# Transposed queries and keys: a pair of heads on the partitions instead of one head in both directions

## The chip, the cores and the metric

The kernel runs on one core of a Trainium2 chip. The metric is the device time of one execution in microseconds, the median of several runs. The engines are TensorE (PE: matmuls and transposes, with its weight loads, PEld, beside them), VectorE (DVE), ScalarE (ACT), GpSimd (POOL) and SyncE (SP), which issues most of the DMAs.

## The reference

One layer of an encoder over 2048 positions with 1024 features, float32. One projection feeds two groups of heads. Group A is gated linear attention with four heads (64 key dimensions, 128 value dimensions), run in both directions over chunks and summed; group B is latent attention with a softmax over all positions. Their outputs are gated, joined, projected and normalised with the residual. What the change touches is the linear attention:

```python
# log_a, one for each direction d in (fwd, bwd):
log_a = log_sigmoid(lr_d @ wg2_d + bg_d) / 16          # (B, S, 4, 64)
def gla_chunked(q, k, v, log_a, strict):               # bwd: on flipped inputs, strict
    b = cumsum(log_a)                                  # inside a chunk of positions
    q_dec, k_dec = q * exp(b), k * exp(-b)
    k_tail = k * exp(b_last - b)
    attn = where(mask, einsum('bhtd,bhsd->bhts', q_dec, k_dec), 0)
    o_intra = attn @ v
    # scan over chunks:
    o_inter = q_dec @ state
    state = state * exp(b_last)[..., None] + einsum('bhsd,bhsv->bhdv', k_tail, v)
    return o_intra + o_inter
o = rms_norm(o_fwd + flip(o_bwd)) * silu(gate)
```

## The kernel before

The kernel has four stages in time: a first sweep over the sequence (`sweep_a`, to about 368 us), a second sweep (`sweep_c`), the softmax attention over four blocks of 512 queries, and the output projection with the norm. Every product of two float32 matrices is made of three matmuls on split values: a high part, written by a ScalarE copy (`hi`, L362 to L367) or a VectorE one, and a low part, a subtraction (`lo`, L369 to L371); `mm3` (L417 to L421) issues high x high, high x low, low x high at lines 419, 420 and 421.

The first sweep takes the 2048 positions in 16 chunks of 128, from the last (c=15, step i=0) to the first (c=0, i=15). For both directions at once it makes the decayed queries and keys of a chunk, its inner attention and its contribution to the state. The order of a chunk's work:

- Products (`products`, tile ipa): the chunk's x against 1056 columns in three groups of 288, 384 and 384 (low rank and q; k and part of v; the rest of v), eight pieces of k-depth 128 each, three matmuls a piece.
- `ga_lr`: the two ScalarE copies and the VectorE subtraction that make the low-rank input lr from the first group; `ga_q2`, `ga_k2`: ScalarE copies of q and k from PSUM.
- `ga_lrT` (L863 to L869): PE transposes lr, ScalarE copies it (lrTs). `ga_z` (L874 to L893): four matmuls make the log decay z (L881), ScalarE (L885, L887, L889) and VectorE (L891) make za of it.
- `ga_sums`: two scans on VectorE (L902 forward, L904 backward) sum za along the chunk, small copies (L908 to L911) take the sums at the chunk's middle and end (cl), L914 subtracts the middle, and ScalarE takes the exponentials E1 (L918) and E2 (L920). `ga_cw` (L924) takes the exponential of cl.
- `ga_q`: PE transposes q (qT, L933), VectorE multiplies by E1 (qd, L936), a DMA stores qd for the second sweep (L937), and by halves of the partitions qd is split into qbh and qbl, each 64 partitions x 512. `ga_k`: kT (L952), kd (L955), its parts kh and kl.
- `ga_kt`: four PE transposes of kd (kt, L969) and the parts kth and ktl. `ga_intra`: the attention scores Ap, chosen by direction into At (ScalarE L986, VectorE L988), its parts Ah and Al. `ga_av`: Op, and oi, stored (L1010). `ga_state`: Up (L1021, L1022), Us (ScalarE L1025, VectorE L1027, GpSimd L1029), stored as su_s (L1030), then the running state Sb (L1035). `ga_bst`: Sm (L1050), stored (L1051).
- Gates (`gate_products`, tile ipg, 512 columns; gs on ScalarE and VectorE) for all chunks but 15, 14 and 0, whose gates come elsewhere.

How work is ordered: chunk i=0 runs in program order. For i=1 to 3 an order written out by hand (`ORDER_A`) holds on all engines. From i=4 a table places stages behind pieces of the products:

```python
STEPS_A = {(0, 4): [("q", "prev"), ("k", "prev")], (1, 3): [("kt", "prev"), ("lrT", "cur")],
           (1, 5): [("z", "cur"), ("cw", "cur")], (1, 7): [("intra", "prev")], (2, 3): [("state", "prev")],
...
```

So q and k of the chunk before are transposed after the fifth piece of the first product group, kt and lrT stand after the fourth piece of the second group, z two pieces later; within this a scheduler of the framework may shift instructions of an engine. The last chunk has its own order at the end of `sweep_a`. PSUM tiles come from three pools of two buffers: ip (ipa, ipg), gp (z, Ap, Op) and tr (transposes and Up). The stores of chunks 0 and 1 (`STORE_POOL`) are issued by GpSimd, all others by SyncE. After the sweep SyncE loads the weights and constants of the second one (L1140), and qd_s, su_s, oi_s and u_s are read back from DRAM chunk by chunk (SU, qdb, oib, ub), which then feed GpSimd's Sf and SU and the matmuls Ob (L1417, L1418).

In all tiles of a direction and head the partitions hold (direction r, dimension d) and the free axis the head h; q and k are copied twice side by side (q2, k2), so that one 128x128 transpose of a head gives it for both directions.

Of the kernel before, what the change touches and what calls it, by code (L numbers as in the profile page):

```python
# [9 lines left out]
F32 = mybir.dt.float32  # L10
F32R = mybir.dt.float32r
I32 = mybir.dt.int32
AF = mybir.ActivationFunctionType
ALU = mybir.AluOpType
# [4 lines left out]
P = 128  # L19
# [4 lines left out]
H = 4  # L24
# [6 lines left out]
TAU_INV = 1.0 / 16.0  # L31
# [323 lines left out]
class K:  # L355
# [413 lines left out]
        yield  # L769

    def ga_q2(self, d):
        d["q2"] = d["g1"].tile([P, H, 2, 64], F32, tag="q2", name=f"q2_{d['c']}", bufs=2)
        self.hi(d["q2"], d["pt", 0][:, 32:288].rearrange("p (h o d) -> p h o d", h=H, o=1).to_broadcast([P, H, 2, 64]))
        yield

    def ga_k2(self, d):
        d["k2"] = d["g1"].tile([P, H, 2, 64], F32, tag="k2", name=f"k2_{d['c']}", bufs=2)
        self.hi(d["k2"], d["pt", 1][:, 0:256].rearrange("p (h o d) -> p h o d", h=H, o=1).to_broadcast([P, H, 2, 64]))
        yield

    def ga_v1(self, d):
# [114 lines left out]
    def ga_sums(self, d):  # L896

        nc, c, za, rmask = self.nc, d["c"], d["za"], d["rmask"]
        V, Ac = nc.vector, nc.scalar
        b = self.t512(d, "E1")  # L900
        f2 = lambda t: t.rearrange("p h t -> p (h t)")
        V.tensor_tensor_scan(f2(b)[0:64], f2(rmask)[0:64], f2(za)[0:64], 0.0, ALU.mult, ALU.add)  # L902
        yield
        V.tensor_tensor_scan(f2(b)[64:128, ::-1], f2(rmask)[64:128, ::-1], f2(za)[64:128, ::-1],  # L904
                             0.0, ALU.mult, ALU.add)
        yield
        cl = d["cl"] = d["g1"].tile([P, 3, H], F32, tag="cl", name=f"cl{c}")
        V.tensor_copy(cl[0:64, 0], b[0:64, :, 63])  # L908
        V.tensor_copy(cl[64:128, 0], b[64:128, :, 64])
        V.tensor_copy(cl[0:64, 2], b[0:64, :, 127])  # L910
        V.tensor_copy(cl[64:128, 2], b[64:128, :, 0])  # L911
        V.tensor_tensor(cl[:, 1], cl[:, 2], cl[:, 0], ALU.subtract)
        yield
        d["zdone"] = V.tensor_tensor(b, b, cl[:, 0, :, None].to_broadcast([P, H, P]), ALU.subtract).ins  # L914
        yield
        E2 = self.t512(d, "E2")
        d.update(E1=b, E2=E2)
        Ac.activation(E2, b, AF.Exp, scale=-TAU_INV)  # L918
        yield
        Ac.activation(b, b, AF.Exp, scale=TAU_INV)  # L920
        yield

    def ga_cw(self, d):
        self.nc.scalar.activation(self.cw[:, d["c"]], d["cl"], AF.Exp, scale=TAU_INV)  # L924
        yield

    def ga_q(self, d):

        nc, c = self.nc, d["c"]
        qbh, qbl = d["qbh"], d["qbl"]  # L930
        qT = d["tr"].tile([P, H, P], F32, tag="tr", name=f"qT{c}")
        for h in range(H):
            nc.tensor.transpose(qT[:, h], d["q2"][:, h].rearrange("p a d -> p (a d)"), self.ident)  # L933
        yield
        qd = self.t512(d, "qd")
        nc.vector.scalar_tensor_tensor(qd, qT, 0.125, d["E1"], ALU.mult, ALU.mult)  # L936
        self.store(c).dma_start(self.qd_s[c], qd.rearrange("p h t -> p (h t)"))  # L937
        yield
        halves = (slice(0, 64), 0), (slice(64, 128), 1)
        for r, j in halves:  # L940
            self.hi(qbh[r, :, j], qd[r])
            yield
        for r, j in halves:
            self.lo(qbl[r, :, j], qd[r], qbh[r, :, j])
            yield

    def ga_k(self, d):

        nc, c = self.nc, d["c"]
        kT = d["tr"].tile([P, H, P], F32, tag="tr", name=f"kT{c}")  # L950
        for h in range(H):
            nc.tensor.transpose(kT[:, h], d["k2"][:, h].rearrange("p a d -> p (a d)"), self.ident)  # L952
        yield
        kd = d["kd"] = self.t512(d, "kd")
        nc.vector.tensor_tensor(kd, kT, d["E2"], ALU.mult)  # L955
        yield
        kh = d["kh"] = self.t512(d, "kh", dt=F32R)
        self.hi(kh, kd)
        yield
        kl = d["kl"] = self.t512(d, "kl", dt=F32R)  # L960
        self.lo(kl, kd, kh)
        yield

    def ga_kt(self, d):

        nc, c = self.nc, d["c"]
        kt = d["tr"].tile([P, H, P], F32, tag="tr", name=f"kt{c}")
        for h in range(H):
            nc.tensor.transpose(kt[:, h], d["kd"][:, h], self.ident)  # L969
        yield  # L970
        kth = d["kth"] = self.t512(d, "kth", dt=F32R)
        self.hi(kth, kt)
        yield
        ktl = d["ktl"] = self.t512(d, "ktl", dt=F32R)
        self.lo(ktl, kt, kth)
        yield

    def ga_intra(self, d):

        nc, c = self.nc, d["c"]  # L980
        Ap = d["gp"].tile([P, H, 2, P], F32, tag="gp", name=f"Ap{c}")
        for h in range(H):
            self.mm3(Ap[:, h], d["kh"][:, h], d["kl"][:, h], d["qbh"][:, h], d["qbl"][:, h])
        yield
        At = self.t512(d, "At")
        nc.scalar.activation(At, Ap[:, :, 1], AF.Copy)  # L986
        yield
        nc.vector.copy_predicated(At, d["mask"][:, None, :].to_broadcast([P, H, P]), Ap[:, :, 0])  # L988
        yield
        Ah = d["Ah"] = self.t512(d, "Ah", dt=F32R)  # L990
        self.hi(Ah, At)
        yield
        Al = d["Al"] = self.t512(d, "Al", dt=F32R)
        self.lo(Al, At, Ah)
        yield
# [949 lines left out]
def layouts(inputs):  # L1945

    g = {k: np.asarray(v) for k, v in inputs.items()}
# [3 lines left out]
    q, k, v, gate, lrf, lrb, cq, ckv, kr, mg = (slice(cols[i], cols[i + 1]) for i in range(10))  # L1951
    cat = lambda *s: np.concatenate([w[:, t] for t in s], axis=1)
    a = {}
# [2 lines left out]
    a["wA"] = cat(lrf, lrb, q, k, v).reshape(NK, P, NA)  # L1956
    a["wB"] = cat(gate, cq, ckv, kr, mg).reshape(NK, P, 1472)
    a["wO"] = g["w_out"][0].reshape(NK, P, D)
    wg = np.zeros((32, H, 2, 64), np.float32)
    wg[0:16, :, 0] = g["gla_wg2_fwd"][0].reshape(16, H, 64)  # L1960
    wg[16:32, :, 1] = g["gla_wg2_bwd"][0].reshape(16, H, 64)
    bg = np.stack([g["gla_bg_fwd"][0].reshape(H, 64), g["gla_bg_bwd"][0].reshape(H, 64)], axis=1)
    wg, bg = wg.reshape(32, H * P), bg.reshape(1, H * P)
    a["wg"] = np.concatenate([wg, wg, wg, bg, bg], axis=0)
    wgm = np.zeros((98, 1), np.float32)
# [17 lines left out]
    a["ident"] = np.eye(P, dtype=np.float32)  # L1983
    a["mask"] = np.triu(np.ones((P, P), np.int32))
    rmask = np.ones((P, H, P), np.float32)
    rmask[0:64, :, 0] = 0.0
    rmask[64:128, :, P - 1] = 0.0
    a["rmask"] = rmask
    invf = (10000.0 ** (-np.arange(32) / 32)).astype(np.float32)
    a["invf"] = np.broadcast_to(invf[None, :], (P, 32))  # L1990
# [20 lines left out]
```

## Time and profile before

| | |
|---|---|
| median of 3 runs | 1307.95 us (1307.42 to 1308.66) |
| the profiled execution | 1308.66 us |
| its span, first to last instruction | 1306.3 us |
| mean granted TensorE clock | 0.997 |
| instructions | 19979 |
| busy: PE, PEld | 1280.9 us, 1130.9 us |
| busy: DVE, ACT, POOL | 958.2, 812.8, 783.6 us |

The page's times are microseconds unless marked ns. A row of a group reads: line, engine, operation, out<-in by the program's names, partitions x elements, x count, then busy time and mean ns of one, then the idle time of the engine just ahead of them and what ended it. Rows of the timeline and of the chain of waits start with the start time and the duration. In a row of the waits stand who waited, for whom, the total in us, how often and the longest. Matmuls are pipelined and their ends are modelled, so neighbours on PE overlap.

### The profile page before, as it was taken

How to read it: one execution, taken by the hardware profiler on the slowest of the kernel's cores; microseconds unless marked ns; L12 is line 12 of the kernel's file. 1: busy time of each engine (PE TensorE's matmuls, PEld its weight loads, DVE VectorE, ACT ScalarE, POOL GpSimd, SP SyncE). 2: the span in 40 equal slices, each digit the busy share in tenths (PEclk: the TensorE clock that was granted, in tenths of full speed). 3: DMA queues.
4: the chain of work that ended last, by engine and by line, in shares of the span. 5: the costliest groups of instructions: out<-in, count | busy, mean ns of one | idle time of the engine just before them, and what ended most of it. 6: DMA issues, size and time to landing. Idle time of an engine off the chain costs nothing.

```text
span 1306.3 us, 19979 instructions
## 1 busy us (share of the span) xinstructions
PE 1280.9 (98%) x7081; PEld 1130.9 (87%) x7081; DVE 958.2 (73%) x1712; ACT 812.8 (62%) x1339; POOL 783.6 (60%) x494
## 2 busy tenths in 40 slices
PE   7999999999999999999999999999999999999997
PEld 7999999999989999999788888888888887887786
DVE  6967774645675455555798888888888888377998
ACT  6764656655575656655688878888888888411110
POOL 0143333242457666672298888889999999934441
PEclk9999999999999999999999999999999999999999
DMA  8131313122475565565501111122123110376563
GB/s 285 61 101 54 94 49 91 55 68 79 132 249 170 193 214 181 178 210 170 145 1 41 41 42 41 41 57 65 58 81 97 41 41 12 119 234 175 195 197 109
DMA packets 107820, 145.81 MB, mean 112 GB/s; under 512 B 17251, under 2 KB 62695, under 8 KB 107721
## 3 DMA queue, kind: packets, MB, share of 16 engines
q1 hardware_dynamic: 99128, 142.41, 35.6%
q0 software_dynamic: 672, 2.10, 0.4%
q8 instruction: 56, 0.92, 0.3%
q10 hardware_dynamic: 7920, 0.03, 0.3%
q14 instruction: 44, 0.35, 0.2%
HBM read 94.14 MB, written 50.36 MB: 111 GB/s over the span
## 4 chain that ended last, share of the span: by engine, by line
PE 83%; DMA 4%; DVE 3%; ACT 2%; POOL 1%; issue 1%; SPq 1%; DVEq 0%; POOLq 0%; ACTq 0%
PE pS L1520 4%; PE o L419 4%; PE o L420 4%; PE o L421 4%; PE pS L1522 4%; PE pS L1523 4%; PE pS L1521 4%; PE pS L1524 4%; PE ipa L419 4%; PE ipa L421 4%; PE ipa L420 4%; PE pz L420 2%; PE pz L419 2%; PE pz L421 2%; PE ipg L419 2%; PE ipg L420 2%
## 5 line engine op out<-in xcount | busy, mean ns | idle before, releaser
L371 POOL TENSOR_TENSOR pl<-s,ph 128x1024 fp32r<-128x1024 f32 x128 | 306.5, 2414 | 58.3 <-ACT ph L365 54.5
L1542 DVE TENSOR_TENSOR rm<-pS,rm 128x512 f32<-128x512 f32 x210 | 144.8, 690 | 36.5 <-ACT s L1529 31.2
L1529 ACT ACTIVATE s<-pS 128x1024 f32<-128x1024 f32 x128 | 131.4, 1027 | 60.6 <-PE pS L1524 51.3
L1566 DVE TENSOR_TENSOR s<-s,mb 128x1024 f32<-128x1024 f32 x128 | 151.2, 1213 | 9.5 <-PE mb L1560 9.3
L1029 POOL TENSOR_TENSOR Us<-Us,cw 128x512 f32<-128x512 f32 x16 | 18.5, 1157 | 227.2 <-DVE Us L1027 175.3
L365 ACT ACTIVATE ph<-s 128x1024 fp32r<-128x1024 f32 x128 | 135.2, 1057 | 17.1 <-PE o L421 16.5
L1570 ACT ACTIVATE s<-s 128x1024 f32<-128x1024 f32 x128 | 131.4, 1050 | 13.7 <-DVE s L1566 13.7
L419 PE MATMUL ipa<-wah,xah 128*128 128x384 f32 (+1 forms) x384 | 131.1, 342 | 6.7 <-ACT wah L365 6.7
L421 PE MATMUL ipa<-wah,xal 128*128 128x384 f32 (+1 forms) x384 | 125.5, 327 | 0.0
L420 PE MATMUL ipa<-wal,xah 128*128 128x384 f32 (+1 forms) x384 | 125.2, 326 | 0.0
L1520 PE MATMUL pS<-qh,ckvT_h 128*128 128x512 f32 x256 | 102.6, 401 | 0.8 <-DVE rm L1542 0.4
L419 PE MATMUL o<-ph,vh 128*128 128x512 f32 x256 | 101.0, 395 | 0.0
L421 PE MATMUL o<-ph,vl 128*128 128x512 f32 x256 | 99.8, 390 | 0.0
L1522 PE MATMUL pS<-qh,ckvT_l 128*128 128x512 f32 x256 | 99.8, 390 | 0.0
L1523 PE MATMUL pS<-rh,krs 128*128 128x512 f32 x256 | 99.8, 390 | 0.0
L1524 PE MATMUL pS<-rl,krs 128*128 128x512 f32 x256 | 99.7, 389 | 0.0
L1521 PE MATMUL pS<-ql,ckvT_h 128*128 128x512 f32 x256 | 99.7, 389 | 0.0
L420 PE MATMUL o<-pl,vh 128*128 128x512 f32 x256 | 99.7, 389 | 0.0
L1593 DVE TENSOR_TENSOR ap<-ap,s 128x512 f32<-128x512 f32 x120 | 83.0, 692 | 2.7 <-ACT s L1570 0.7
L371 POOL TENSOR_TENSOR ol<-of,oh 128x512 fp32r<-128x512 f32 x32 | 42.9, 1343 | 66.9 <-ACT oh L365 66.9
L419 PEld LDWEIGHTS ipa<-wah,xah 128*128 128x128 f32 x384 | 73.7, 192 | 7.9 <-ACT wah L365 7.0
L419 PE MATMUL pz<-xch,wzh 128*128 128x256 f32 x256 | 74.8, 292 | 0.0
(325 smaller groups left out, 3858.0 us busy)
## 6 DMA issues: line engine op xcount, KB each, us to landing
xcf<-xT_dram SPq DMA_DIRECT2D x16, 512.0 KB, 4.9
xr<-x_dram SPq DMA_DIRECT2D x16, 512.0 KB, 6.6
out_dram<-rr SPq DMA_DIRECT2D x32, 256.0 KB, 2.0
xaf<-xT_dram SPq DMA_DIRECT2D x14, 512.0 KB, 4.2
oib<-oi_s SPq DMA_DIRECT2D x16, 256.0 KB, 4.4
qdb<-qd_s SPq DMA_DIRECT2D x16, 256.0 KB, 4.6
SU<-su_s SPq DMA_DIRECT2D x16, 256.0 KB, 4.9
ub<-u_s SPq DMA_DIRECT2D x16, 256.0 KB, 4.7
```

What stands on the lines that cost most here:

```text
L365: return nc.scalar.activation(dst, src, AF.Copy).ins
L371: return e.tensor_tensor(dst, src, hi.bitcast(F32), ALU.subtract).ins
L419: mm(out, ah, bh, start=start, stop=False)
L420: mm(out, ah, bl, start=False, stop=False)
L421: mm(out, al, bh, start=False, stop=stop)
L1520: mm(ps[:, e], kh, qh, start=True, stop=False)
L1521: mm(ps[:, e], kh, ql, start=False, stop=False)
L1522: mm(ps[:, e], kl, qh, start=False, stop=False)
L1523: mm(ps[:, e], kr, rh, start=False, stop=False)
L1524: mm(ps[:, e], kr, rl, start=False, stop=True)
L1542: V.tensor_tensor(d["rm"], src[:, e], d["rm"], ALU.max)
L1566: V.tensor_tensor(s, s, d["mb"][:, None, :].to_broadcast([P, 2, QB]), ALU.subtract)
```

## The change

The partitions of the transposed tiles now hold (head g of a pair, dimension d), and the free axis (direction r, pair q). q2 and k2 are copied once, 256 elements a partition instead of 512, and q and k take two transposes of 128x128 each instead of four. qd and kd multiply by the decay of both directions by reading the two transposed tiles twice. The scans become one per direction over 128 partitions and 256 elements instead of 64 partitions and 512; the small copies have 128x2 instead of 64x4. What is read by the stages behind has its old layout: the exponentials of cl are written by four ScalarE instructions of 64 partitions x 6 (with other partitions in than out) instead of one of 128 x 12, qd is stored by four DMAs (64 partitions, two runs of 512 bytes each) instead of one (128 partitions, 2 KB each), kth and ktl are written in another order of their four blocks of 64, and Ap is read by direction. The four transposes of kd stay. The weights wg and bias bg and the mask of the scans are laid out accordingly in the host's preparation.

In the built programs PE has 64 matmul instructions fewer, ScalarE 48 instructions more, SyncE 42 and GpSimd 6 DMA issues more. The order on each engine is otherwise the same but for a few places: from i=4 on one product matmul (L419) stands between kt and lrT on PE; ScalarE issues two cw, E2, two cw, E1, Us in place of cw, Us, E2, E1; GpSimd issues the four stores of chunk 0's qd ahead of Sm.

```diff
@@ -769,13 +769,13 @@
         yield
 
     def ga_q2(self, d):
-        d["q2"] = d["g1"].tile([P, H, 2, 64], F32, tag="q2", name=f"q2_{d['c']}", bufs=2)
-        self.hi(d["q2"], d["pt", 0][:, 32:288].rearrange("p (h o d) -> p h o d", h=H, o=1).to_broadcast([P, H, 2, 64]))
+        d["q2"] = d["g1"].tile([P, 2, P], F32, tag="q2", name=f"q2_{d['c']}", bufs=2)
+        self.hi(d["q2"].rearrange("p a d -> p (a d)"), d["pt", 0][:, 32:288])
         yield
 
     def ga_k2(self, d):
-        d["k2"] = d["g1"].tile([P, H, 2, 64], F32, tag="k2", name=f"k2_{d['c']}", bufs=2)
-        self.hi(d["k2"], d["pt", 1][:, 0:256].rearrange("p (h o d) -> p h o d", h=H, o=1).to_broadcast([P, H, 2, 64]))
+        d["k2"] = d["g1"].tile([P, 2, P], F32, tag="k2", name=f"k2_{d['c']}", bufs=2)
+        self.hi(d["k2"].rearrange("p a d -> p (a d)"), d["pt", 1][:, 0:256])
         yield
 
     def ga_v1(self, d):
@@ -899,16 +899,16 @@
         V, Ac = nc.vector, nc.scalar
         b = self.t512(d, "E1")
         f2 = lambda t: t.rearrange("p h t -> p (h t)")
-        V.tensor_tensor_scan(f2(b)[0:64], f2(rmask)[0:64], f2(za)[0:64], 0.0, ALU.mult, ALU.add)
-        yield
-        V.tensor_tensor_scan(f2(b)[64:128, ::-1], f2(rmask)[64:128, ::-1], f2(za)[64:128, ::-1],
+        V.tensor_tensor_scan(f2(b[:, 0:2]), f2(rmask[:, 0:2]), f2(za[:, 0:2]), 0.0, ALU.mult, ALU.add)
+        yield
+        V.tensor_tensor_scan(f2(b[:, 2:4])[:, ::-1], f2(rmask[:, 2:4])[:, ::-1], f2(za[:, 2:4])[:, ::-1],
                              0.0, ALU.mult, ALU.add)
         yield
         cl = d["cl"] = d["g1"].tile([P, 3, H], F32, tag="cl", name=f"cl{c}")
-        V.tensor_copy(cl[0:64, 0], b[0:64, :, 63])
-        V.tensor_copy(cl[64:128, 0], b[64:128, :, 64])
-        V.tensor_copy(cl[0:64, 2], b[0:64, :, 127])
-        V.tensor_copy(cl[64:128, 2], b[64:128, :, 0])
+        V.tensor_copy(cl[:, 0, 0:2], b[:, 0:2, 63])
+        V.tensor_copy(cl[:, 0, 2:4], b[:, 2:4, 64])
+        V.tensor_copy(cl[:, 2, 0:2], b[:, 0:2, 127])
+        V.tensor_copy(cl[:, 2, 2:4], b[:, 2:4, 0])
         V.tensor_tensor(cl[:, 1], cl[:, 2], cl[:, 0], ALU.subtract)
         yield
         d["zdone"] = V.tensor_tensor(b, b, cl[:, 0, :, None].to_broadcast([P, H, P]), ALU.subtract).ins
@@ -921,7 +921,11 @@
         yield
 
     def ga_cw(self, d):
-        self.nc.scalar.activation(self.cw[:, d["c"]], d["cl"], AF.Exp, scale=TAU_INV)
+        cw = self.cw[:, d["c"]].rearrange("p n (q g) -> p n q g", g=2)
+        for r in range(2):
+            for g in range(2):
+                self.nc.scalar.activation(cw[64 * r:64 * r + 64, :, :, g], d["cl"][64 * g:64 * g + 64, :, 2 * r:2 * r + 2],
+                                          AF.Exp, scale=TAU_INV)
         yield
 
     def ga_q(self, d):
@@ -929,12 +933,17 @@
         nc, c = self.nc, d["c"]
         qbh, qbl = d["qbh"], d["qbl"]
         qT = d["tr"].tile([P, H, P], F32, tag="tr", name=f"qT{c}")
-        for h in range(H):
-            nc.tensor.transpose(qT[:, h], d["q2"][:, h].rearrange("p a d -> p (a d)"), self.ident)
+        for p in range(2):
+            nc.tensor.transpose(qT[:, p], d["q2"][:, p], self.ident)
         yield
         qd = self.t512(d, "qd")
-        nc.vector.scalar_tensor_tensor(qd, qT, 0.125, d["E1"], ALU.mult, ALU.mult)
-        self.store(c).dma_start(self.qd_s[c], qd.rearrange("p h t -> p (h t)"))
+        two = lambda t: t.rearrange("p (r q) t -> p r q t", r=2)
+        nc.vector.scalar_tensor_tensor(two(qd), qT[:, None, 0:2].to_broadcast([P, 2, 2, P]), 0.125, two(d["E1"]),
+                                       ALU.mult, ALU.mult)
+        dst = self.qd_s[c].rearrange("(r d) (q g t) -> r g d q t", r=2, q=2, g=2)
+        for r in range(2):
+            for g in range(2):
+                self.store(c).dma_start(dst[r, g], qd[64 * g:64 * g + 64, 2 * r:2 * r + 2])
         yield
         halves = (slice(0, 64), 0), (slice(64, 128), 1)
         for r, j in halves:
@@ -948,11 +957,12 @@
 
         nc, c = self.nc, d["c"]
         kT = d["tr"].tile([P, H, P], F32, tag="tr", name=f"kT{c}")
-        for h in range(H):
-            nc.tensor.transpose(kT[:, h], d["k2"][:, h].rearrange("p a d -> p (a d)"), self.ident)
+        for p in range(2):
+            nc.tensor.transpose(kT[:, p], d["k2"][:, p], self.ident)
         yield
         kd = d["kd"] = self.t512(d, "kd")
-        nc.vector.tensor_tensor(kd, kT, d["E2"], ALU.mult)
+        two = lambda t: t.rearrange("p (r q) t -> p r q t", r=2)
+        nc.vector.tensor_tensor(two(kd), kT[:, None, 0:2].to_broadcast([P, 2, 2, P]), two(d["E2"]), ALU.mult)
         yield
         kh = d["kh"] = self.t512(d, "kh", dt=F32R)
         self.hi(kh, kd)
@@ -968,11 +978,13 @@
         for h in range(H):
             nc.tensor.transpose(kt[:, h], d["kd"][:, h], self.ident)
         yield
+        by_head = lambda t: t.rearrange("p h (r d) -> p r h d", r=2)
+        src = kt.rearrange("p (r q) (g d) -> p r (q g) d", r=2, g=2)
         kth = d["kth"] = self.t512(d, "kth", dt=F32R)
-        self.hi(kth, kt)
+        self.hi(by_head(kth), src)
         yield
         ktl = d["ktl"] = self.t512(d, "ktl", dt=F32R)
-        self.lo(ktl, kt, kth)
+        self.lo(by_head(ktl), src, by_head(kth))
         yield
 
     def ga_intra(self, d):
@@ -983,9 +995,10 @@
             self.mm3(Ap[:, h], d["kh"][:, h], d["kl"][:, h], d["qbh"][:, h], d["qbl"][:, h])
         yield
         At = self.t512(d, "At")
-        nc.scalar.activation(At, Ap[:, :, 1], AF.Copy)
-        yield
-        nc.vector.copy_predicated(At, d["mask"][:, None, :].to_broadcast([P, H, P]), Ap[:, :, 0])
+        of_dir = lambda r: Ap[:, 2 * r:2 * r + 2].rearrange("p q g t -> p (q g) t")
+        nc.scalar.activation(At, of_dir(1), AF.Copy)
+        yield
+        nc.vector.copy_predicated(At, d["mask"][:, None, :].to_broadcast([P, H, P]), of_dir(0))
         yield
         Ah = d["Ah"] = self.t512(d, "Ah", dt=F32R)
         self.hi(Ah, At)
@@ -1956,10 +1969,10 @@
     a["wA"] = cat(lrf, lrb, q, k, v).reshape(NK, P, NA)
     a["wB"] = cat(gate, cq, ckv, kr, mg).reshape(NK, P, 1472)
     a["wO"] = g["w_out"][0].reshape(NK, P, D)
-    wg = np.zeros((32, H, 2, 64), np.float32)
-    wg[0:16, :, 0] = g["gla_wg2_fwd"][0].reshape(16, H, 64)
-    wg[16:32, :, 1] = g["gla_wg2_bwd"][0].reshape(16, H, 64)
-    bg = np.stack([g["gla_bg_fwd"][0].reshape(H, 64), g["gla_bg_bwd"][0].reshape(H, 64)], axis=1)
+    wg = np.zeros((32, 2, H * 64), np.float32)
+    wg[0:16, 0] = g["gla_wg2_fwd"][0]
+    wg[16:32, 1] = g["gla_wg2_bwd"][0]
+    bg = np.stack([g["gla_bg_fwd"][0], g["gla_bg_bwd"][0]])
     wg, bg = wg.reshape(32, H * P), bg.reshape(1, H * P)
     a["wg"] = np.concatenate([wg, wg, wg, bg, bg], axis=0)
     wgm = np.zeros((98, 1), np.float32)
@@ -1983,8 +1996,8 @@
     a["ident"] = np.eye(P, dtype=np.float32)
     a["mask"] = np.triu(np.ones((P, P), np.int32))
     rmask = np.ones((P, H, P), np.float32)
-    rmask[0:64, :, 0] = 0.0
-    rmask[64:128, :, P - 1] = 0.0
+    rmask[:, 0:2, 0] = 0.0
+    rmask[:, 2:4, P - 1] = 0.0
     a["rmask"] = rmask
     invf = (10000.0 ** (-np.arange(32) / 32)).astype(np.float32)
     a["invf"] = np.broadcast_to(invf[None, :], (P, 32))
```

## The prediction

> **What bounds the kernel now.** I read the page first: engines, then the chain that ended last. TensorE (PE) is busy for 98% of the span and holds 83% of the chain; no other engine has more than 4% of it.
>
> ```profile
> span 1306.3 us, 19979 instructions
> PE 1280.9 (98%) x7081; PEld 1130.9 (87%) x7081; DVE 958.2 (73%) x1712; ACT 812.8 (62%) x1339; POOL 783.6 (60%) x494
> PE 83%; DMA 4%; DVE 3%; ACT 2%; POOL 1%; issue 1%; SPq 1%; DVEq 0%; POOLq 0%; ACTq 0%
> ```
>
> That is an average, so next comes the table of windows over the first sweep, which is the only stage that changes (0 to about 368 us). Its columns are window, sum, then busy us with instruction counts of PE, PEld, DVE, ACT, POOL, then the granted clock, DMA share and GB/s.
>
> ```profile
> 20.00:40.00 20.00, 19.60 (x131) 19.17 (x130) 15.46 (x28) 16.09 (x35) 0.00 (x0) 1.00 0.63 206
> 40.00:60.00 20.00, 19.57 (x126) 18.42 (x125) 19.13 (x31) 12.79 (x26) 5.49 (x4) 1.00 0.18 60
> 200.00:250.00 50.00, 49.65 (x316) 46.88 (x315) 28.63 (x53) 32.16 (x61) 15.87 (x11) 1.00 0.26 70
> 350.00:400.00 50.00, 48.21 (x299) 43.14 (x297) 33.88 (x60) 36.48 (x72) 29.22 (x31) 1.00 0.74 234
> ```
>
> In 200 to 250 us PE works 49.65 of 50 at granted clock 1.00 while VectorE (DVE) and ScalarE (ACT) have 18 us or more free. In 20 to 60 us PE lacks 0.83 us in all, and in 40 to 60 VectorE is almost full too. At the sweep's end (350 to 400) PE lacks 1.8. So in this sweep a PE instruction removed is time removed, unless a waiting PE instruction takes it back. PE's waits, asked for 0 to 60 us (first three rows) and 60 to 420 (last two):
>
> ```profile
> PE ipa L419 <- ACT wah L365: 6.7, 2, 5.8
> PE Up L1022 <- DVE ktl L371: 0.4, 1, 0.4
> PE z L881 <- ACT lrTs L365: 0.4, 1, 0.4
> ...
> PE Ob L1418 <- POOL qlb L371: 0.8, 1, 0.8
> PE Ap L421 <- DVE kl L371: 0.7, 2, 0.3
> ```
>
> The 6.7 us are the first weights, which the change doesn't touch. The rest is small, each once or twice in a sweep.
>
> **Term 1: the transposes.** Each of 16 chunks loses two of four transposes of q and two of four of k: 64 PE instructions. What is one worth? The rows are the tile qT (all 64), then PE's timeline in one chunk, then the chain of waits near the sweep's end.
>
> ```profile
> L933 PE MATMUL qT<-ident,q x64: 270/272/293, 31.6 to 350.2; 128*128 128x128 f32 x64
> ...
> 200.25 0.60 PE L933 MATMUL qT<-ident,q 128*128 128x128 f32 x4
> 200.68 0.60 PE L952 MATMUL kT<-ident,k 128*128 128x128 f32 x4
> ...
> 335.90 0.44 PE qT L933 x4
> ```
>
> A transpose lasts 272 ns, but four of them last 0.60 us, and the next four start 0.43 us after the first: they overlap in the pipeline. What one occupies is the spacing, 0.44 / 4 = 0.109 us (from 0.43 to 0.44 for four). So a chunk loses 4 x 0.109 = 0.435 us of PE, and the sweep 16 x 0.435 = 7.0 us, if all of it lies on the path.
>
> The Trainium skill, TensorE: Matmul & The Clock Gate, Part 4: PE-mode transpose, puts a 128x128 transpose at about 275 ns in a kernel. The duration here, 272, agrees, the spacing does not; 64 at 275 would be 17.6 us, and that is a rival below only for the chance that the spacing is misread.
>
> **Term 2: what VectorE takes back.** In a chunk from the fifth on, PE does q's and k's transposes after piece 4 of the first product group, and kt (transposes of kd) and then lrT after piece 3 of the second. lrT needs VectorE's lr, which stands at the end of a queue that starts with qd, and qd waits for the last transpose of q:
>
> ```profile
> 200.88 0.69 DVE L936 SCALAR_TENSOR_TENSOR qd<-qT,E 128x512 f32<-128x512 f32 x1 [3.89 <-PE qT L933]
> 201.49 0.68 DVE L1482 TENSOR_TENSOR gs<-ipg,gs 128x512 f32<-128x512 f32 x1
> 202.09 0.68 DVE L955 TENSOR_TENSOR kd<-kT,E 128x512 f32<-128x512 f32 x1
> 202.69 1.39 DVE L371 TENSOR_TENSOR qbl<-qd,qbh 64x512 fp32r<-64x512 f32 x2
> 204.11 0.69 DVE L371 TENSOR_TENSOR kl<-kd,kh 128x512 fp32r<-128x512 f32 x1
> 204.72 0.18 DVE L371 TENSOR_TENSOR lr<-ipa,lr 128x32 fp32r<-128x32 f32 x1
> ...
> 204.27 0.34 PE L421 MATMUL ipa<-wah,xal 128*128 128x384 f32 x1
> 204.44 0.60 PE L969 MATMUL kt<-ident,kd 128*128 128x128 f32 x4
> 205.05 0.29 PE L869 MATMUL lrT<-ident,lr 128*98 128x128 f32 x1
> ```
>
> VectorE has no gap from 200.88 to lr's end at 204.90. kt starts at 204.44, so lrT could start at 204.44 + 0.435 = 204.88 and starts at 205.05: a stall of about 0.17 us that the list of waits doesn't show. With two transposes, qd starts 2 x 0.109 = 0.217 earlier, so lr too; PE arrives 0.435 earlier. Alone that lets the stall grow by 0.22, and half the gain is gone. But the order of the built kernels shows one product matmul more between kt and lrT in these chunks, 128x384, which occupies 0.17 (from 204.27 to 204.44). It fills the stall: 0.17 - 0.217 + 0.435 - 0.17 = 0.22 instead of 0.17. So a chunk gains 0.435 - 0.05 = 0.39 us (0.217 without the filler, 0.435 if VectorE is not late). qd, gs, kd, qbl, kl keep their sizes: qd and kd read two transposed tiles twice by a broadcast, 512 elements a partition as now, taken at 0.69 and 0.68 (no row shows a broadcast from PSUM; the end below is the same, above I allow the 1.39 / 2 of the strided qbl, which is the same again).
>
> **Term 3: smaller operations.** These rows are groups by shape: VectorE's scan, its sum for comparison, then ScalarE's copies and cw.
>
> ```profile
> L904 DVE TENSOR_TENSOR_SCAN E<-rmask,za 64x512 f32<-64x512 f32 x16 | 20.5, 1279 | 0.5
> L914 DVE TENSOR_TENSOR E<-E,cl 128x512 f32<-128x512 f32 x16 | 10.9, 683 | 0.0
> L365 ACT ACTIVATE q<-ipa 128x512 f32<-128x512 f32 x16 | 9.6, 598 | 11.8 <-DVE lr L371 10.9 <-PE ipa L421 0.7 <-DVE wal L371 0.2
> L365 ACT ACTIVATE VV<-ipa 128x384 fp32r<-128x384 f32 x16 | 7.6, 478 | 1.5 <-PE ipa L421 1.5
> L365 ACT ACTIVATE VV<-ipa 128x128 fp32r<-128x128 f32 x16 | 4.4, 273 | 1.9 <-PE Op L1004 1.9
> L924 ACT ACTIVATE cw<-cl 128x12 f32<-128x12 f32 x16 | 3.2, 198 | 1.5 <-DVE cl L912 1.5
> ```
>
> Two scans go from 64x512 to 128x256. If time follows the elements of a partition, each takes some 0.6 instead of 1.28 (0.6 to 1.28), up to 1.3 us less VectorE a chunk. The Trainium skill, DVE: opcode table, instruction layouts, handler registers and perf-mode slots, section 6, says that this scan runs at half throughput; 1279 against 683 of a plain 512 agrees, and by it a half scan costs about a plain one. q2 and k2 copy 256 instead of 512: between 273 (128) and 478 (384), 0.375, so 0.22 less each on ScalarE. cw becomes four instructions of 64x6: 4 x 0.198 = 0.79 at most, 0.6 more. ScalarE thus ends at +0.15 a chunk or less. In 200 to 250 us both engines have over 17 us free, and E and cw are wanted only a chunk later: nothing on the path, as cover of several us stands there. The permuted writes kth and ktl and the permuted reads of Ap keep 512 elements; the strided qbl at 1.39 / 2 against kl at 0.69 says that a stride is free here. If kth did cost 0.1 more, lrTs and z behind it on ScalarE would be late by that, but the copy of q ahead of kth gets 0.22 shorter. In the first chunks the scans can pay: VectorE is at 19.13 of 20 in 40 to 60 us, and the stalls at z and Up are 0.4 each. I count 0 there (at most 0.8).
>
> **Term 4: stores.** qd goes out by four DMAs of 64 rows of two 512-byte runs instead of one of 128 rows. The first row is the issue on SyncE's queue, the others are GpSimd's timeline at the end, where chunks 0 and 1 are stored, and the chain.
>
> ```profile
> L937 SPq DMA_DIRECT2D qd_s<-qd x14: 320/383/392, 33.1 to 315.3; - x14
> ...
> 353.33 1.30 POOL L1035 TENSOR_TENSOR Sb<-Sb,Us 64x512 f32<-64x512 f32 x1
> 354.71 1.37 POOL L1050 TENSOR_TENSOR Sm<-Sb,cw 64x512 f32<-64x512 f32 x1
> 356.94 0.55 POOL L937 DMA_DIRECT2D qd_s<-qd  x1
> 363.66 1.03 POOL L1029 TENSOR_TENSOR Us<-Us,cw 128x512 f32<-128x512 f32 x1 [4.86 <-DVE Us L1027]
> 365.57 0.56 POOL L833 DMA_DIRECT2D u_s<-gs  x1
> ...
> 364.99 4.44 DMA su_s<-Us
> 369.56 0.33 SPq L1140
> ...
> 373.86 4.65 DMA SU<-su_s
> ```
>
> SyncE: 3 x 0.383 = 1.15 us more of issuing in a chunk of 22.5; queued behind are loads of x for later chunks and stores, none wanted in that time. GpSimd: 3 x 0.55 = 1.65 us more for chunk 0, ahead of Sm and its store in the built order; the next thing that matters is Us at 363.66, with 4.86 us idle before it. That hides it. Uncovered, the 1.65 would go on whole: su_s lands at 369.43, SyncE's next loads are issued from 369.56, SU is read back from 373.86, and from there the chain goes on to qlb and the wait of Ob (0.8). So 0 here, between +1 (the denser DMA traffic at the boundary, share 0.74, lands su_s later) and -1.1 (the stalls Ap 0.3 and Ob 0.8 go).
>
> **The sum.** First four chunks, ordered by hand: 4 x 0.435 = 1.74. Eleven chunks: 11 x 0.39 = 4.3. The last: 0.4. Together 6.5 us, taken from the profiled execution of 1308.66 us (span 1306.3 and 2.4 around it): 1302.2. That execution stands 0.7 above the median of the three runs, so on the median the forecast is 1307.95 - 6.5 = 1301.4 us. A measurement here tells 0.2% or 2.6 us from no change, so "faster" begins at 1305.3.
>
> **Rivals.**
> 1. VectorE keeps half: without effect of the filler a chunk gains 0.217, so 1.74 + 11 x 0.217 + 0.4 = 4.5 us, 1303.4. For it: VectorE's queue without a gap. Against: the filler in the order. Chance 0.16.
> 2. The shorter scans and copies also empty VectorE and ScalarE where PE waits: z, Up, Ap, Ob (0.4 + 0.4 + 0.7 + 0.8 at most, from the waits), with 0.435 in every chunk: 7.0 + 2.3 = 9.3 at the extreme, some 8.6, 1299.3. For it: 40 to 60 us. Against: four separate places must all give. Chance 0.12.
> 3. Slower: GpSimd's four stores of chunk 0 wait for one another's landing, 4.44 each, ahead of Sm. From Sb's end at 354.6 they would last 4 x 5.0 us to 374.6, Sm and its store to 376.5, so Us would start 13 us after 363.66. By the chain that delay reaches Ob whole: 13 less 6.5, about 1314. It decides once the stores and Sm outlast the stretch from 354.6 to 363.7. Against: u_s is issued at 365.57, 0.58 after su_s at 364.99, though su_s needs 4.44 to land. Chance 0.03.
> 4. No change: the PE time comes back as waits on VectorE in each chunk (the broadcast reads or permuted writes cost 0.4 a chunk more, all on the queue up to lr or z): 1306 to 1308.5. Against: equal element counts. Chance 0.06.
> 5. Transposes worth 272 ns each: 17.4 us, 1290.5. Against: the spacing. Chance 0.01.
>
> The forecast has 0.62, with 1300.2 to 1302.8 as its own range. Rivals 1 and 2 lie within 1298.9 to 1304.5, which leaves out 3, 4, 5 and the tails, less than 2 in 10. Faster: 0.62 + 0.16 + 0.12 + 0.01 less 0.01 for tails, 0.90; same 0.06; slower 0.04.
>
> **What would show it.** Right: qT and kT groups of x2 at 0.22 in the chain, lrT about 0.2 late behind one product matmul after kt, a chunk's period 0.39 shorter, scans at about 0.6, Us of chunk 0 at its place relative to Up, Ob's wait near 0.8. Wrong: lrT or z late by 0.4 or more (rivals 1 and 4), qd, kd, kth or ktl over 0.75, GpSimd's four stores further apart than 0.6 us.

## The result, and the profile after

| | before | after |
|---|---|---|
| median, six runs each | 1308.3 us | 1303.0 us |
| the profiled execution | 1308.66 us | 1303.84 us |
| its span | 1306.3 us | 1301.6 us |

The ratio is 0.9961, with a 95% interval of 0.9951 to 0.9971: 5.1 us faster by the ratio, 5.3 by the medians. The forecast was 1301.4, 6.5 us faster, with a range of 1298.9 to 1304.5; sign and range hold, and the gain is a fifth smaller than forecast.

The page after, its head:

```profile
span 1301.6 us, 19963 instructions
PE 1273.0 (98%) x7017; PEld 1122.8 (86%) x7017; DVE 927.6 (71%) x1712; ACT 817.4 (63%) x1387; POOL 785.4 (60%) x500
```

PE lost 64 instructions and 7.9 us of busy time; the span fell by 4.7. So something was given back. Where shows when the sweep is cut at its lrT matmuls. The rows are the tile lrT between 85 and 345 us, chunks i=4 to 15, before and then after; what counts is the first and the last start.

```profile
L869 PE MATMUL lrT<-ident,lr x12: 271/287/288, 92.6 to 340.5; 128*98 128x128 f32 x12
```

```profile
L869 PE MATMUL lrT<-ident,lr x12: 270/287/288, 89.9 to 333.8; 128*98 128x128 f32 x12
```

Eleven chunks took 247.9 us and take 243.9: 4.0 us less (4.3 forecast for eleven). By starts read in the trace a regular chunk in the middle of the sweep went from 22.51 to 22.09 us. Three of the eleven gained less: the first 0.2, and two irregular ones (25.5 and 19.9 us before) 0.4 together. Now one such chunk on PE after (timeline, 195 to 202 us):

```profile
195.83 0.38 PE L937 MATMUL qT<-ident,q 128*128 128x128 f32 x2
196.05 0.38 PE L961 MATMUL kT<-ident,k 128*128 128x128 f32 x2
...
197.36 0.29 PE L421 MATMUL ipa<-wah,xal 128*128 128x288 f32 x1
197.59 0.44 PE L419 MATMUL ipa<-wah,xah 128*128 128x384 f32 x1
197.87 0.34 PE L420 MATMUL ipa<-wal,xah 128*128 128x384 f32 x1
...
199.81 0.60 PE L979 MATMUL kt<-ident,kd 128*128 128x128 f32 x4
200.16 0.42 PE L419 MATMUL ipa<-wah,xah 128*128 128x384 f32 x1
200.42 0.28 PE L869 MATMUL lrT<-ident,lr 128*98 128x128 f32 x1
200.46 0.42 PE L420 MATMUL ipa<-wal,xah 128*128 128x384 f32 x1
200.72 0.34 PE L421 MATMUL ipa<-wah,xal 128*128 128x384 f32 x1
```

and VectorE in the same chunk:

```profile
196.25 0.69 DVE L941 SCALAR_TENSOR_TENSOR qd<-qT,E 128x512 f32<-128x512 f32 x1 [3.68 <-PE qT L937]
196.86 0.68 DVE L1495 TENSOR_TENSOR gs<-ipg,gs 128x512 f32<-128x512 f32 x1
197.46 0.68 DVE L965 TENSOR_TENSOR kd<-kT,E 128x512 f32<-128x512 f32 x1
...
199.48 0.69 DVE L371 TENSOR_TENSOR kl<-kd,kh 128x512 fp32r<-128x512 f32 x1
200.09 0.18 DVE L371 TENSOR_TENSOR lr<-ipa,lr 128x32 fp32r<-128x32 f32 x1
```

The pair of transposes occupies 0.22 (195.83 to 196.05) instead of 0.43. The product matmul stands between kt and lrT. lrT still starts 0.15 us after lr's end (200.27 to 200.42; 204.90 to 205.05 before), but PE loses next to nothing there: it comes 0.26 after that product, and the product behind lrT, which waits for nothing, also takes 0.26 to its follower (200.46 to 200.72). So the stall of 0.22 that was forecast at lrT is some 0.01 there. It lies earlier, where none was expected: the first matmul of the second group starts 0.23 us after its predecessor (197.36 to 197.59; 0.14 at the same place before, 202.17 to 202.31), and the next one 0.28 after that (0.20 before; 0.175 between such products further on), some 0.2 together. Its PSUM buffer is the one that VectorE's gs reads, and gs ends at 197.54, because it stands behind qd. So VectorE's queue now stops PE at gs. From qT to lrT the transposes took 0.435 away, the filler added 0.175, and the distance fell from 4.80 to 4.59, so the stalls on this stretch grew by some 0.05, as in the forecast.

Groups by shape, 0 to 380 us, VectorE and then ScalarE:

```profile
L904 DVE TENSOR_TENSOR_SCAN E<-rmask,za 128x256 f32<-128x256 f32 x16 | 11.7, 734 | 0.0
L941 DVE SCALAR_TENSOR_TENSOR qd<-qT,E 128x512 f32<-128x512 f32 x16 | 11.0, 689 | 41.2 <-PE qT L937 41.0 <-issue 0.2
L902 DVE TENSOR_TENSOR_SCAN E<-rmask,za 128x256 f32<-128x256 f32 x16 | 10.9, 684 | 0.1
```

```profile
L365 ACT ACTIVATE q<-ipa 128x256 f32<-128x256 f32 x16 | 6.1, 384 | 11.4 <-DVE lr L371 10.8 <-PE ipa L421 0.5 <-DVE wal L371 0.2
L927 ACT ACTIVATE cw<-cl 64x6 f32<-64x6 f32 x64 | 13.0, 203 | 2.5 <-DVE cl L912 1.8
```

A scan costs 0.68 to 0.73 (0.6 forecast), qd with its broadcast read 0.689 as before, the copy of q 0.384 (0.375 forecast), a cw 0.203 (0.198).

What was given back stands at the very end. PE's waits from 1120 us on, before and then after:

```profile
PE pmb L419 <- DVE rr L1926: 3.1, 1, 3.1
```

```profile
PE pmb L419 <- DVE rr L1939: 5.3, 1, 5.3
```

PE's one long wait in the output projection grew by 2.2 us, some 800 us behind the last changed instruction. The chain of waits there, before and then after:

```profile
1184.79 0.38 SPq L1850
1185.22 14.26 DMA gr<-gm_s
1199.50 0.92 SPq L1853
1200.46 7.79 DMA xr<-x_dram
1208.38 0.70 DVE rr L1926
1209.22 0.47 PE pmb L419
```

```profile
1178.58 0.53 SPq L1864
1179.16 15.58 DMA gr<-r_s
1194.76 7.78 DMA xr<-x_dram
1202.62 0.40 issue
1203.02 0.70 DVE rr L1939
1203.86 0.77 PE pmb L419
```

PE waits for VectorE's residual rr, rr for a load of x, and that load's issue on SyncE for transfers that take 14 to 16 us to land. SyncE issues the same list of DMAs in the same order here in both kernels. It isn't SyncE's loads alone that land later: so does a store that ScalarE issues among them, before and then after (the last number is the time from issue to landing in us):

```profile
r_s<-rc ACTq DMA_DIRECT2D x1, 2.0 KB, 11.0
```

```profile
r_s<-rc ACTq DMA_DIRECT2D x1, 2.0 KB, 13.7
```

SyncE's next load of gr waits for that landing, 2.7 us before and 5.5 after.

### The profile page after: what moved, and what is told of

Read it like the earlier page. It is cut to its first block, busy times and chain, and to the rows that moved or that the text cites. A ratio compares the mean times of both kernels' runs of the same rounds, so it can differ in the third digit from the quotient of the medians.

```text
span 1301.6 us, 19963 instructions
## 1 busy us (share of the span) xinstructions
PE 1273.0 (98%) x7017; PEld 1122.8 (86%) x7017; DVE 927.6 (71%) x1712; ACT 817.4 (63%) x1387; POOL 785.4 (60%) x500
## 4 chain that ended last, share of the span: by engine, by line
PE 83%; DMA 4%; DVE 3%; ACT 3%; POOL 2%; issue 2%; SPq 0%; DVEq 0%; POOLq 0%; ACTq 0%
PE o L419 4%; PE o L420 4%; PE pS L1533 4%; PE o L421 4%; PE pS L1535 4%; PE pS L1536 4%; PE pS L1537 4%; PE pS L1534 4%; PE ipa L419 4%; PE ipa L421 3%; PE ipa L420 3%; PE pz L420 2%; PE pz L419 2%; PE pz L421 2%; PE ipg L419 2%; PE ipg L420 2%
## 5 line engine op out<-in xcount | busy, mean ns | idle before, releaser
L419 PE MATMUL ipa<-wah,xah 128*128 128x384 f32 (+1 forms) x384 | 131.2, 342 | 6.9 <-ACT wah L365 6.4
L419 PE MATMUL o<-ph,vh 128*128 128x512 f32 x256 | 101.0, 395 | 0.0
L419 PEld LDWEIGHTS ipa<-wah,xah 128*128 128x128 f32 x384 | 72.9, 190 | 9.9 <-ACT wah L365 6.6
L419 PE MATMUL pz<-xch,wzh 128*128 128x256 f32 x256 | 74.8, 292 | 0.0
```

The source lines that it names most:

```text
L419: mm(out, ah, bh, start=start, stop=False)
```

## The experiments

Theory A: the transposes are the gain, PE's time and nothing else. Rival C: the shorter scans and copies are. Where the late wait comes from had theories of its own: chance (a part of A), a shorter sweep (B), the stores of qd (D), something else of the new layout (E). Each kernel was timed against the kernel before on the same chip; "before again", "after again", "four transposes again" and "two transposes in the old kernel" ran on one chip, the four rows from "one store" on a second, the last four on a third. Two kernels compute other values: "two transposes in the old kernel" leaves out two heads' transposed q and k, and "one store" keeps the rows of qd in an order that the second sweep doesn't read. The table has for each the median, the ratio with its interval, and from its one trace the first four chunks (first lrT to that of i=4), the eleven chunks from there, the wait of pmb, and the stretch from the last matmul of tile o to the end, all in us.

| kernel | median | ratio (95%) | first four | eleven | pmb | end |
|---|---|---|---|---|---|---|
| before, profiled | 1308.3 | | 74.2 | 247.9 | 3.1 | 156.3 |
| before again | 1308.08 | 1.0004 (0.9995 to 1.0012) | 75.0 | 248.0 | 3.0 | 155.5 |
| after, profiled | 1303.0 | 0.9961 (0.9951 to 0.9971) | 73.5 | 243.9 | 5.3 | 159.2 |
| after again | 1303.52 | 0.9967 (0.9953 to 0.9981) | 73.1 | 243.8 | 5.2 | 158.6 |
| four transposes again | 1308.91 | 1.0013 (1.0004 to 1.0022) | 74.6 | 247.0 | 5.1 | 159.4 |
| two transposes in the old kernel | 1301.7 | 0.9958 (0.9945 to 0.9972) | 73.9 | 244.1 | 2.5 | 154.1 |
| one store | 1299.27 | 0.9934 (0.9921 to 0.9948) | 73.0 | 243.9 | 2.9 | 156.0 |
| old kernel, store split | 1309.23 | 1.0007 (0.9999 to 1.0016) | 75.0 | 247.9 | 3.8 | 157.4 |
| scans twice | 1305.26 | 0.9977 (0.9967 to 0.9987) | 73.4 | 244.3 | 4.1 | 157.6 |
| one piece earlier | 1303.24 | 0.9960 (0.9946 to 0.9975) | 75.2 | 241.6 | 4.3 | 158.7 |
| earlier from i=5 | 1301.68 | 0.9950 (0.9938 to 0.9963) | 73.5 | 241.6 | 4.6 | 157.9 |
| two stores | 1303.8 | 0.9967 (0.9954 to 0.9979) | 73.5 | 243.8 | 3.7 | 157.8 |
| earlier and two stores | 1300.97 | 0.9947 (0.9933 to 0.9961) | 73.5 | 241.5 | 3.8 | 158.0 |
| stores of qd by GpSimd | 1300.59 | 0.9945 (0.9933 to 0.9958) | 72.7 | 243.8 | 2.9 | 156.4 |

**Both kernels again.** No edit; the question is whether the late wait is chance.

> The kernel before, unchanged, for a second trace. Theory A (the gain is the sweep's, and the output projection's wait for its loads of x, 3.1 us before and 5.3 after, is chance): steady chunk period 22.51 us again, the wait of pmb for rr anywhere between 2 and 6 us, the first lrT within 2 us of 18.40; time 1308 within 1. Rival B (the later part of the kernel takes 2 us of the gain back whenever the sweep is shorter): pmb waits 3.1 again, within 0.5.

> The changed kernel, unchanged, for a second trace. Theory A: period 22.09 us again, pmb's wait not tied to 5.3; 1302 to 1304. Rival B: pmb waits 5.3 again, within 0.5, and the whole kernel gains 5 us where the sweep gains 7.

It is not: 3.1 and 3.0 before, 5.3 and 5.2 after. The part of theory A that called it chance fell. What does scatter is the start: the first lrT came at 18.4 and 17.0 us before, 16.4 and 16.1 after, and between 16.2 and 17.4 in the ten traces below.

**Four transposes again**, in the changed kernel:

```diff
-        for p in range(2):
-            nc.tensor.transpose(qT[:, p], d["q2"][:, p], self.ident)
+        for p in range(4):
+            nc.tensor.transpose(qT[:, p], d["q2"][:, p % 2], self.ident)
```

and kT likewise.

> The changed kernel with each of its q and k transposes issued twice, so four of each again; the second pair is read by nobody. Theory A (the transposes are the gain): steady period back to about 22.5 us, sweep 6 to 7 us longer than the changed kernel's, total 1308 to 1309. Rival C (the shorter scans and copies on VectorE and ScalarE are the gain): at least half of the gain stays, 1303 to 1306.

The gain goes, and the rest of the change alone is slower than the kernel before, 1.0013 (1.0004 to 1.0022). The eleven chunks keep only 0.9 of 4.0 us (a regular chunk takes 22.40, 0.11 less than before), and pmb waits 5.1 with a sweep as long as before, to within 2 us. That also ends rival B: a shorter sweep isn't what lengthens the wait.

**Two transposes in the old kernel:**

```diff
-        for h in range(H):
+        for h in range(2):
             nc.tensor.transpose(qT[:, h], d["q2"][:, h].rearrange("p a d -> p (a d)"), self.ident)
...
-        nc.vector.scalar_tensor_tensor(qd, qT, 0.125, d["E1"], ALU.mult, ALU.mult)
+        two = lambda t: t.rearrange("p (r q) t -> p r q t", r=2)
+        nc.vector.scalar_tensor_tensor(two(qd), qT[:, None, 0:2].to_broadcast([P, 2, 2, P]), 0.125, two(d["E1"]),
+                                       ALU.mult, ALU.mult)
```

and kT, kd likewise.

> The kernel before with only the first two of the four transposes of q and of k, their two tiles read twice; scans, copies and stores stay the old ones (two heads' transposed values are left out). Theory A: steady period 22.09 us and the whole gain, 1302 to 1304; the order has the product matmul between kt and lrT here too. Rival C: at most half of the gain, 1305 to 1308.

Here the transposes alone give at least the whole gain (0.9958), with old scans, old copies and one store; pmb waits 2.5. Its trace, tile lrT from 85 to 345 us:

```profile
L869 PE MATMUL lrT<-ident,lr x12: 272/288/290, 90.5 to 334.6; 128*98 128x128 f32 x12
```

244.1 us for eleven chunks, a regular one 22.12. Theory A stands, C falls as the source of the gain: the rest of the change is worth 0.03 us a chunk beside two transposes (22.12 against 22.09), 0.11 beside four.

**One store** in the changed kernel:

```diff
-        for r in range(2):
-            for g in range(2):
-                self.store(c).dma_start(dst[r, g], qd[64 * g:64 * g + 64, 2 * r:2 * r + 2])
+        self.store(c).dma_start(self.qd_s[c], qd.rearrange("p h t -> p (h t)"))
```

> The changed kernel with qd stored by one DMA of 128 rows again (the stored rows stand in another order than the second sweep reads, so its results are other values). The traces so far show the output projection's first wait (pmb for its load of x) at 2.5 to 3.1 us in three kernels with one store a chunk and at 5.1 to 5.3 in three with four. Theory D (the number of DMAs that were issued before shifts the output projection's transfers): the wait is 3 us or less again, total 2 us under the changed kernel, 1300 to 1302. Theory E (the stores are innocent, something else of the new layout does it): the wait stays at 5 us and the total at 1303.

**The old kernel with its store split:**

```diff
-        self.store(c).dma_start(self.qd_s[c], qd.rearrange("p h t -> p (h t)"))
+        for n in range(4):
+            self.store(c).dma_start(self.qd_s[c][32 * n:32 * n + 32], qd[32 * n:32 * n + 32].rearrange("p h t -> p (h t)"))
```

> The kernel before with its store of qd split into four DMAs of 32 rows, nothing else. Theory D: pmb waits 5 us instead of 3, total 2 us over the kernel before, 1309 to 1311, sweep unchanged at 22.51 a chunk. Theory E: pmb waits 3 us, total as before within 0.7. Under both the stores cost the sweep itself nothing; a longer chunk period would show that they do.

PE's wait, with one store in the changed kernel, and with the split store in the old one:

```profile
PE pmb L419 <- DVE rr L1937: 2.9, 1, 2.9
```

```profile
PE pmb L419 <- DVE rr L1927: 3.8, 1, 3.8
```

With one store the wait is 2.9 again and the total 1299.27, some 4 us under the changed kernel against the same kernel before (0.9934 and 0.9967): the stores took it, theory E falls. The split adds less: 3.8, the end 1 to 2 us longer, the ratio's interval just at 1. So theory D is right that the stores do it. Whether four with 2 KB runs cost less than four with 512 bytes is not shown: on this chip the two kernels below with 512-byte runs waited 4.1 and 4.3, and the 5.1 and 5.2 of "four transposes again" and "after again" come from another. In both the sweep is untouched (243.9, 247.9).

**Scans twice** in the changed kernel (each `tensor_tensor_scan` line written twice).

> The changed kernel with each of the two scans issued twice, so that the scans take VectorE as long as before the change. Theory A (scans lie beside PE's work in the steady chunks): period 22.09, total within 1 us of the changed kernel. Rival C (shorter scans are a part of the gain): period over 22.2 or the first four chunks over 1 us longer, total 1304.5 or more.

The eleven chunks grow by 0.4 and the first four don't: in the steady sweep the scans lie almost wholly beside PE's work. The total is 1 to 2 us longer nevertheless, and its trace has 2.3 us more between the last lrT and the last Op. This row, the windows of that trace, tells why that can't be laid on the scans alone:

```profile
333.00:365.00 32.00, 30.54 (x169) 26.69 (x168) 23.15 (x41) 19.54 (x41) 12.36 (x18) 0.95 0.71 234
```

The granted clock was 0.95 in that stretch and 1.00 in the changed kernel's. What the scans are worth at the sweep's end stays open.

**One piece earlier**, one place in the table:

```diff
-STEPS_A = {(0, 4): [("q", "prev"), ("k", "prev")], (1, 3): [("kt", "prev"), ("lrT", "cur")],
+STEPS_A = {(0, 3): [("q", "prev"), ("k", "prev")], (1, 3): [("kt", "prev"), ("lrT", "cur")],
```

> The changed kernel with the q and k stage one product piece earlier (after the fourth piece of the first group instead of the fifth, one place in the table). In the changed kernel's steady chunk PE stalls some 0.13 us at the second group's first product (it waits for VectorE's gs, which stands behind qd) and 0.09 us at lrT: together the 0.22 that was forecast at lrT alone. Theory F (VectorE's queue, which starts with q's transposes, sets both stalls): 0.4 us earlier they go, period 21.9, total 2 us less, about 1301. Rival G (gs or a later operation then holds PE in the same way): period 22.05 or more, total unchanged within 0.7.

**Earlier from i=5 on** (the same table for i >= 5, the old one for i=4):

> The changed kernel with the q and k stage one product piece earlier from step i=5 on only; step 4, where the earlier stage made kt wait 1.4 us for kd, keeps its place. Theory F (the earlier stage removes VectorE's stalls in the steady chunks and the loss of the run before was the junction at step 4): period 21.86, first four chunks 73.3 us as in the changed kernel, total 1301 or less, 1 to 2.5 us under the changed kernel. Rival G (the junction only moves a chunk on): total 1303.

PE's waits from 60 to 340 us in the first of the two, and the tile lrT (85 to 345 us) in the second:

```profile
PE kt L979 <- DVE kd L965: 1.4, 1, 1.4
PE ipa L419 <- DVE gs L1495: 0.6, 1, 0.6
```

```profile
L870 PE MATMUL lrT<-ident,lr x12: 272/272/273, 90.3 to 331.9; 128*98 128x128 f32 x12
```

Theory F holds: a chunk of 21.86 us, 0.22 less than after, which is the stall that VectorE's queue held (all but wholly at gs, by the reading above, and not 0.09 of it at lrT), and lrT follows kt's last transpose by 0.109, its spacing. The edit moved more than q and k: in the built order kd now stands ahead of gs on VectorE, and three of kt's four transposes stand on PE ahead of the second group's first product, in the time that it waits for gs. At step 4, where the hand-written order ends, the earlier stage cost 1.4 us at kt; left out there, the loss of the first four chunks goes too. Total 1301.68. Against the kernel before the interval of this run (0.9938 to 0.9963) overlaps those of the first placement and of the changed kernel, so the totals alone don't tell them apart; the sweeps in the traces do.

**Two stores**, in rows that hold the heads as (g, q), which the second sweep's Ob matmuls then read so:

```diff
...
+        dst = self.qd_s[c].rearrange("(r d) (g f) -> g d r f", r=2, g=2)
+        for g in range(2):
+            self.store(c).dma_start(dst[g], qd[64 * g:64 * g + 64].rearrange("d (r q) t -> d r (q t)", r=2))
```

> The changed kernel with qd stored by two DMAs a chunk (64 partitions, two runs of 1 KB) instead of four (two runs of 512 bytes); the scratch rows hold the heads as (g, q) and the second sweep's Ob matmuls index them so. Theory D (what was issued before on the queue costs the output projection's transfers time, more with more and shorter runs): pmb's wait 3 to 4.5 us, the stretch behind the last o matmul 156 to 158 us instead of 158.9, total 1300 to 1302.5. Theory E': four against one is a matter of chance in how the DMAs fall, with two it may be anything from 3 to 6 us.

**Earlier and two stores:**

> Both edits together: q and k one piece earlier from i=5 on, and two stores a chunk. If the two gains lie in different stretches they add up: sweep 2 us shorter, the stretch behind the last o matmul 1 to 3 us shorter than the changed kernel's, total 1298 to 1300.5. If not, no better than the better of the two.

**Stores of qd by GpSimd:**

```diff
-                self.store(c).dma_start(dst[r, g], qd[64 * g:64 * g + 64, 2 * r:2 * r + 2])
+                self.nc.gpsimd.dma_start(dst[r, g], qd[64 * g:64 * g + 64, 2 * r:2 * r + 2])
```

> The changed kernel with all 64 stores of qd issued by GpSimd, so that SyncE's queue has the issues of a kernel without them (14 fewer than before the change). Theory D with the hardware queue as the place: pmb waits 3 us or less, the stretch behind the last o matmul 156 us or less. If it is the stored runs themselves (512 bytes to the scratch tensor), not the queue: 158 to 159 as in the changed kernel. The sweep may lose if GpSimd's issues, 4 times 0.55 us a chunk, delay Us.

Two stores leave pmb at 3.7 and the total where it was (1303.8): the lower wait brought nothing that the total shows. In both kernels with two stores PE waits 1.5 us for kl at Ap at the sweep's end, against 0.7 in the changed kernel; why was not looked for. With the edits together the total is 1300.97, that of the earlier stage, within its interval. GpSimd's stores are the same transfers with the same 512-byte runs, and with them pmb waits 2.9:

```profile
PE pmb L419 <- DVE rr L1939: 2.9, 1, 2.9
```

On the same chip the kernel with the earlier stage and four stores, 56 of 64 by SyncE, waited 4.6. So it isn't the runs by themselves but who issues them: what SyncE issued in the sweep changes how transfers fall at the end. GpSimd's four issues a chunk cost the sweep nothing (243.8). At 1300.59 (0.9945), it is level with the two kernels of the earlier stage, the fastest here that compute all of it. Its interval overlaps the changed kernel's, so the gain from moving the stores is read from its trace and from "one store", whose interval doesn't overlap; whether it adds to the earlier stage was not run.

## Why the prediction was right, and where it was not

The sums below take the two traces of each kernel together (means of spans 1305.9 and 1300.8, so 5.2 us).

- **Term 1, a transpose is worth its spacing, 0.109 us.** Right: the groups of x4 became x2 at 0.22, and the experiments with the transposes alone give the whole gain. At 272 ns each (rival 5) it would have been 17 us. The 275 ns of the Trainium skill (TensorE: Matmul & The Clock Gate, Part 4: PE-mode transpose) agree with a row's duration, 271 in the changed kernel, and not with what a transpose was worth here.
- **Term 2, VectorE takes 0.05 of 0.435 back in a steady chunk.** Right in size: a regular chunk gained 0.42 (0.39 forecast), and eleven 4.1 us (4.3), as three gained less. Wrong in place: the forecast put the whole stall of 0.22 at lrT, where some 0.01 of it is; the rest is at the second group's first two products, behind gs. The step that failed is that only the tail of VectorE's queue was followed to PE; gs in its middle holds PE too. Rival 1 needed the filler not to work, and it did.
- **The first four chunks: 1.74.** Measured 74.64 to 73.32, 1.3. From one lrT to the next the four gained 0.6, 0.2, 0.5 and 0.0, not 0.435 each. The first holds the stall at z, which was 0.4 and 1.2 in the two traces before, 0.8 and 0.5 after. In the fourth, where the hand-written order ends, PE has a wait in both changed traces that it didn't have before, again for gs:

```profile
PE ipa L419 <- DVE gs L1495: 0.5, 1, 0.5
```

- **The start**, ahead of the first lrT, came 1.4 us earlier, which no term holds. The two traces before differ by as much among themselves (18.4 and 17.0), and the old kernel with its store split starts at 16.7, so this is taken for chance.
- **The sweep's end: 0.4.** Measured 0.7 from the last lrT to the last Op. The stall at Ob was 0.8 as before.
- **Term 3.** Sizes right within 0.13 us, and next to nothing on the path in the steady sweep (0.03 us a chunk beside two transposes). That a halved scan would cost about what a plain operation of 512 does, by the rule of the Trainium skill (DVE: opcode table, instruction layouts, handler registers and perf-mode slots, section 6), is what the rows show: 684 and 734 against 684 for L914.
- **Term 4, the stores cost nothing.** Wrong. In the sweep it held: GpSimd's four issues took 2.30 us, one behind the other, and Us still came after 3.56 us of idle time (rival 3 fell):

```profile
347.84 2.30 POOL L946 DMA_DIRECT2D qd_s<-qd  x4
350.00 1.22 POOL L1063 TENSOR_TENSOR Sm<-Sb,cw 64x512 f32<-64x512 f32 x1
...
356.21 1.04 POOL L1042 TENSOR_TENSOR Us<-Us,cw 128x512 f32<-128x512 f32 x1 [3.56 <-DVE Us L1040]
```

  But the step "queued behind are loads of x for later chunks and stores, none wanted in that time" looked only at the sweep. The stretch behind the last o matmul went from 155.9 to 158.9, 3.0 us, of which pmb's wait is 2.2. Attention, from the first pS to the last matmul of o, was 0.7 us shorter (533.5 to 532.8); over all fourteen traces it lies between 532.8 and 533.8, at 532.8 in the old kernel with its store split too, so this is taken for chance.

Added up: start -1.4, first four -1.3, eleven -4.1, end of the sweep -0.7, attention -0.7, output projection +3.0: -5.2. The one term that was missed, 3.0, is more than the difference between forecast and result; against it stand the start's 1.4 and attention's 0.7, which the forecast did not count on either. The terms of the sweep held, 6.1 against 6.4, which the forecast calls 6.5. Without the start and attention the gain would have been 3.1 us and the time about 1305, above the range: that the total held is in part luck.

What stays open is how the stores reach so far. In the two traces before, SyncE's issues and their order at the end are those of the changed kernel, and no transfer of the sweep is still under way there. The wait was 2.5 to 3.1 us in the five traces with SyncE's old number of DMAs or fewer, 3.7 to 5.3 in the nine with more. The same five traces have ScalarE's store r_s<-rc landing after 11.0 to 11.4 us, six of the nine after 12.1 to 13.7, so in these the delay shows on another queue too. The two with two stores have no record of it. In the old kernel with its store split it lands after 10.7, but one issue of out_dram holds SyncE for 6.0 us there. What carries the delay from the sweep to the end was not measured.

## What to carry to other kernels

Where transposes follow one another on PE, price one at the spacing of their starts, not at its duration, and then follow every operation of the queue that starts with their result, not only its last, to the matmul that waits for it. An operation that is free where it stands isn't free everywhere: here three more stores a chunk cost nothing that shows in 360 us of sweep and 3 us in a stage 800 us later where PE waits for a load, and moving them to another queue took 2.5 of these back in its one trace. After a change that shortens PE's way to a wait, move the stage that feeds the wait by the same amount; that was worth 2 us more in the sweep than the change alone.

## What the runs showed of the hardware that was not expected

- The same 64 stores, with the same bytes and runs, left a wait in a much later stage at 5.2 and 5.3 us where SyncE issued 56 of them (5.1 with four transposes again, 4.1 to 4.6 in the variants on the second and third chip), and at 2.9 where GpSimd issued all.
- Late in the kernel, beside a store that ScalarE issues (r_s from rc, 128x4), SyncE's loads of 256 KB took 14 to 16 us to land (gr<-gm_s 14.26, gr<-r_s 15.58), against a load of x of twice that size at 7.8.
- A scan over 256 elements of 128 partitions took 684 to 734 ns, little more than half of 1208 to 1279 for 512 elements of 64 partitions: its time follows the elements of a partition, not their total number.
